# A two-layer attention trunk: layer 0's opening in five rounds instead of four, with 1024 merge-gate columns moved into it

## The chip, the cores and the metric

The kernel runs on one core of one Trainium2 chip. The metric is device time in microseconds (us) for one execution; the median of 3 runs of the kernel before is 2167.09 us (2164.69 to 2167.59). The engines are called PE (TensorE), DVE (VectorE), ACT (ScalarE), POOL (GpSimd) and SP (SyncE, which issues nearly all loads here).

## The reference, cut to what matters

Two layers (DEPTH = 2) act on x of 256 rows and 2048 features. Each layer does, in fp32:

```
mod = c @ w_ada + b_ada                      # one row; shift, scale, gate of 2048 each
u = layer_norm(x) * (1 + scale) + shift      # "adaLN"
proj = u @ w_in                              # split into the inputs of three branches and merge_logit
o_a, o_b, o_c = MLA, forgetting and stick-breaking attention on parts of proj
branches = (o_n * silu(g_n)) @ w_branch[n]   # n = 0, 1, 2
merged = sum over n of sigmoid(merge_logit[n]) * branches[n]
x = layer_norm(ALPHA * x + gate * (merged @ w_out)) * ln_g + ln_b
```

So the scale and shift must be summed from w_ada (2048 x 4096 for these two) before the first product of u with w_in, and they are needed feature by feature: feature tile k (128 features, 16 tiles) of u needs only the 128 columns of shift and scale that belong to it.

## The kernel before

An fp32 product is made of three on PE (`three`, lines 264 to 266): both operands are split into a high and a low part, ACT rounds the weights to `whi` (line 235), DVE subtracts for `wlo` (line 236), and PE adds hi*hi, hi*lo and lo*hi. The rows stand in two tiles t of 128. Weights come in pieces of 1 MiB through the four buffers `raw` of the pool wpool; the products of 512 columns are summed in PSUM banks `acc`, small things in two banks `att`.

**The opening of layer 0** (lines 601 to 710) has to fetch shift and scale while it works. It takes the feature tiles four at a time, in rounds q = 0 to 3. `ada_pieces(q, ...)` fetches the 1024 columns of shift and scale for four tiles in 8 pieces of 1 MiB (`raw_s`, line 623). DVE adds each of the 16 rows of a partition, times c, into `ada_s` (`accumulate`, lines 332 and 334), 16 sums of 1024 elements. For the first round, pieces 1, 3 and 5 are summed on PE instead, c as the stationary operand (line 635). Then PE sums over partitions against a column of ones (line 645), DVE adds the bias (`mod`, line 647), and `modulate` transposes the normalised rows `xn`, applies shift and scale on ACT (line 418) and splits the result into `uhi` and `ulo` (lines 421 and 422).

In each round, the tiles that are ready are multiplied with 3912 columns of w_in: two units of the product `first` (1024 columns, PSUM kept open over all rounds) and six blocks by `group_piece` (lines 653 to 684): two of 420 columns (`sum_b`), four of 512, which are the merge gate of branch 0 (`merged`). A block's PSUM result is copied to SBUF by ACT in round 0 (line 679) and added by DVE after that (line 681). The pieces of the next round's shift and scale are interleaved with this work, and the last block of a round is held back behind the next tiles' modulation.

**After it** come the MLA projections (`cqh` times w_uq and w_ukv), the eight MLA heads (`scores`, line 509; `attention_head`, lines 473 to 481; `attend`, lines 487 to 500), the transposes and splits of the heads' outputs (`transposed_split`, line 518, giving `yhi` and `ylo`), and the branch products with `yhi`. The heads use two PSUM banks in turn: scores, then transposed probabilities, then output. In layer 0, `merge_gate(l, 1, 0, ...)`, the first 1024 columns of branch 1's merge gate, is called right behind the MLA attention and does not depend on it:

```
            if l == 0 and n < 2:
                ahead = sig_tile(("ada", "sig")[n])
                sigs[1, n] = merge_gate(l, 1, n, ahead)
```

A scheduler sets the order of the instructions on each engine when the kernel is built, and each engine then runs its list in that order. It may move later work ahead of earlier work where buffers allow.

Of the kernel before, what the change touches and what calls it, by code (L numbers as in the profile page):

```python
# [43 lines left out]
def trunk(  # L44
# [202 lines left out]
    def half_pairs(raw):  # L247

        pairs = []
        for j in range(2):  # L250
            hi = wpool.tile([P, 2, 512], F32R, tag="whi", name="whi")
            lo = wpool.tile([P, 2, 512], F32R, tag="wlo", name="wlo")
            split_weights(raw[:, 2 * j:2 * j + 2], hi, lo)
            pairs += [(hi[:, 0], lo[:, 0]), (hi[:, 1], lo[:, 1])]
        return pairs
# [138 lines left out]
    def normalise_row(src, dst, t, mean):  # L394

        nm = small.tile([P, 1], F32, tag="nm", name="nm")
        nc.vector.tensor_scalar(nm, mean, -1.0, None, op0=ALU.mult)
        ss = small.tile([P, 1], F32, tag="ss", name="ss")
        nc.scalar.activation(dst, src[:, t], AF.Square, bias=nm, accum_out=ss)
        rs = rsqrt(ss, LN_EPS, 1.0 / D)  # L400
        nc.vector.tensor_tensor(out=nm, in0=nm, in1=rs, op=ALU.mult)
        for i in range(4):
            s = slice(i * 512, (i + 1) * 512)
            if i % 2 == 0:
                state["xn"] = nc.vector.tensor_scalar(
                    dst[:, s], src[:, t, s], mean, rs, op0=ALU.subtract, op1=ALU.mult)
            else:
                nc.scalar.activation(dst[:, s], src[:, t, s], AF.Identity, bias=nm, scale=rs)

    def modulated(l, xt_n, k0, um):  # L410

        ps = att_tile().rearrange("p (k s) -> p k s", k=4)
        for j in range(4):
            nc.tensor.transpose(ps[:, j], xt_n[:, (k0 + j) * P:(k0 + j + 1) * P], ident)
        sh, sc = mods[l][:, 0], mods[l][:, 1]
        for j in range(4):
# [7 lines left out]
    def modulate(l, xn, uhi, ulo, k0, t):  # L424
        um = tmp.tile([P, 4, P], F32, tag="t512", name="um")
        modulated(l, xn[t], k0, um)
        split_act(um, uhi[t][:, k0:k0 + 4], ulo[t][:, k0:k0 + 4])
# [118 lines left out]
    for l in range(DEPTH):  # L546
# [57 lines left out]
        if l == 0:  # L604
            sum_b = big.tile([P, NT, 2, 420], F32, tag="qT", name="sum_b")
            groups = []
            for h, parts in enumerate(([(win, CH, 420)], [(win, CH + 420, 412), (win, F0, H)])):
                groups.append((parts, [sum_b[:, t, h] for t in range(NT)],
                               lambda t, s, h=h: evac_a1(t, h, s)))
            for h in range(4):  # L610
                groups.append(([(win, M0 + h * 512, 512)], (h, ),
                               lambda t, s: nc.scalar.activation(s, s, AF.Tanh, scale=0.5)))

            ada_s = big.tile([P, 2, 2, 512], F32, tag="ada", name="ada_s")

            def ada_pieces(q, on_pe):
                acc = ada_s[:, q % 2]
                rows, merge_rows = {}, []

                def piece(u):  # L620
                    raw = wpool.tile([P, 2, 2, 512], F32, tag="raw", name="raw_s")
                    for m in range(2):
                        nc.sync.dma_start(
                            out=raw[:, :, m],
                            in_=w_ada[0].rearrange("(p k) n -> p k n", p=P)[
                                :, 2 * u:2 * u + 2, m * D + q * 512:m * D + (q + 1) * 512])
                    for j in range(2):
                        kk = 2 * u + j
                        if u not in on_pe:
                            accumulate(acc, raw[:, j], kk)  # L630
                            continue
                        for m in range(2):
                            if kk == 2 * on_pe[0]:
                                rows[m] = acc_tile()
                            nc.tensor.matmul(rows[m][:1], c_sb[:, kk:kk + 1], raw[:, j, m],
                                             start=kk == 2 * on_pe[0], stop=kk == 2 * on_pe[-1] + 1)
                            if kk == 2 * on_pe[-1] + 1:
                                merge_rows.append(m)
                    if u == 7:
                        for m in merge_rows:  # L640
                            nc.vector.tensor_tensor(out=acc[:1, m], in0=acc[:1, m], in1=rows[m][:1], op=ALU.add)
                        ps = att_tile()
                        for m in range(2):
                            for k in range(4):
                                nc.tensor.matmul(ps[:, 4 * m + k:4 * m + k + 1], acc[:, m, k * P:(k + 1) * P], ones,
                                                 start=True, stop=True)
                        nc.vector.tensor_tensor(
                            out=mods[0][:, :, 4 * q:4 * q + 4], in0=ps[:, :8].rearrange("p (m k) -> p m k", m=2),
                            in1=bT[0][:, :2, 4 * q:4 * q + 4], op=ALU.add)

                return [lambda u=u: piece(u) for u in range(8)]

            def group_piece(q, parts, sums, done):
                if len(sums) == 1:
                    sums = [merged[:, t, sums[0] * 512:(sums[0] + 1) * 512] for t in range(NT)]
                raw = wpool.tile([P, 4, 512], F32, tag="raw", name="raw_g")
                w = 0
                for src, c0, n in parts:
                    nc.sync.dma_start(
                        out=raw[:, :, w:w + n],  # L660
                        in_=src[q * 512:(q + 1) * 512, c0:c0 + n].rearrange("(k p) n -> p k n", p=P))
                    w += n
                pairs = []
                for j in range(2):
                    hi = wpool.tile([P, 2, 512], F32R, tag="whi", name="whi")[:, :, :w]
                    lo = wpool.tile([P, 2, 512], F32R, tag="wlo", name="wlo")[:, :, :w]
                    nc.scalar.activation(hi, raw[:, 2 * j:2 * j + 2, :w], AF.Copy)  # L667
                    nc.vector.tensor_tensor(  # L668
                        out=lo, in0=raw[:, 2 * j:2 * j + 2, :w], in1=hi.bitcast(F32), op=ALU.subtract)
                    pairs += [(hi[:, 0], lo[:, 0]), (hi[:, 1], lo[:, 1])]  # L670
                for t in range(NT):
                    ps = acc_tile()[:, :w]
                    for j, (hi, lo) in enumerate(pairs):
                        ah, al = uhi[t][:, 4 * q + j], ulo[t][:, 4 * q + j]
                        nc.tensor.matmul(ps, ah, hi, start=j == 0, stop=False)  # L675
                        nc.tensor.matmul(ps, ah, lo, start=False, stop=False)  # L676
                        nc.tensor.matmul(ps, al, hi, start=False, stop=j == 3)  # L677
                    if q == 0:
                        nc.scalar.activation(sums[t], ps, AF.Copy)
                    else:  # L680
                        nc.vector.tensor_tensor(out=sums[t], in0=sums[t], in1=ps, op=ALU.add)  # L681
                    if q == 3:
                        done(t, sums[t])

            for i, f in enumerate(ada_pieces(0, (1, 3, 5))):
                f()
                if i == 0:
                    for t in range(NT):
                        nc.sync.dma_start(out=xt[:, t], in_=x_rows[:, t])
# [365 lines left out]
```

## Time and profile before

| | |
|---|---|
| median of 3 runs | 2167.09 us |
| the profiled execution's own time | 2165.88 us |
| its span, first to last instruction | 2164.2 us |
| mean granted PE clock | 0.989 |
| PE busy | 2083.5 us, 96% |
| DVE busy | 1419.8 us, 66% |
| ACT busy | 985.2 us, 46% |
| moved by DMA | 481.05 MB, mean 222 GB/s |

A line of the timeline has the start in us, the duration, the engine, the line of the code, the operation, what it writes and reads, a count, and in brackets the idle time ahead of it and what ended that. A busy time overlaps where one matmul starts before the last has drained, so a product's price is read from start to start. A line of the stretches has the stretch, its length, then each engine's busy time (with the count) for PE, PEld (weight loads), DVE, ACT and POOL, and at the end the granted clock, the DMA share and GB/s. A group's line has busy time, mean ns of one, and the idle time before it. A wait's line has us in total, how often, and the longest.

### The profile page before, as it was taken

Reading aid. Unit: us, or ns where it says so; the run is one execution under the profiler, and the core shown is the slowest. Engines: PE = TensorE matmul, PEld = TensorE weight load, DVE = VectorE, ACT = ScalarE, POOL = GpSimd, SP = SyncE. Lnnn points to the kernel's source line nnn. Section 1 sums busy time; section 2 is a strip of 40 time slices with the busy share of each in tenths; the row PEclk is TensorE's granted clock in tenths of the full one; section 3 lists DMA queues with packets and bytes.
Section 4 is the critical chain, followed back from the end, with each engine's and each line's share of the span. In section 5 each row is a group of like instructions: output and inputs, shape, how many; then the busy total and the mean of one; then the engine's idle time right before and its main releaser. Section 6 shows DMA issues by size and latency. Waiting matters only on the chain. (4 is left out here: it accounts for less than half of the span.)

```text
span 2164.2 us, 24761 instructions
## 1 busy us (share of the span) xinstructions
PE 2083.5 (96%) x9568; PEld 1694.0 (78%) x9568; DVE 1419.8 (66%) x1951; ACT 985.2 (46%) x1289; POOL 14.3 (1%) x71
## 2 busy tenths in 40 slices
PE   4999999999999999999999999999999999999996
PEld 2777878888788888787848888888778888878885
DVE  6798855676658767876666755555665544466566
ACT  4435644344453445634435644444444444464441
POOL 0000000000000000000000000000000000000000
PEclk8999999999999999999999999999999999999998
DMA  8997545787648877788425646666655555555652
GB/s 313 329 330 264 175 129 174 269 299 291 207 148 298 315 262 279 281 296 308 159 106 187 224 136 233 233 229 219 232 175 175 181 193 191 195 175 195 193 196 97
DMA packets 139894, 481.05 MB, mean 222 GB/s; under 512 B 14704, under 2 KB 18944, under 8 KB 129536
## 3 DMA queue, kind: packets, MB, share of 16 engines
q1 hardware_dynamic: 135344, 464.69, 62.1%
q0 software_dynamic: 2080, 14.70, 1.7%
q8 instruction: 75, 1.23, 0.2%
q10 hardware_dynamic: 2352, 0.08, 0.1%
q14 instruction: 43, 0.35, 0.0%
HBM read 475.21 MB, written 4.23 MB: 222 GB/s over the span
## 5 line engine op out<-in xcount | busy, mean ns | idle before, releaser
L236 DVE TENSOR_TENSOR wlo<-raw,whi 128x1024 fp32r<-128x1024 f32 (+2 forms) x622 | 751.0, 1212 | 556.2 <-ACT whi L235 555.4
L235 ACT ACTIVATE whi<-raw 128x1024 fp32r<-128x1024 f32 (+2 forms) x622 | 650.4, 1050 | 770.6 <-PE acc L266 719.0
L265 PE MATMUL acc<-wlo,uhi 128*128 128x512 f32 (+1 forms) x1824 | 719.1, 394 | 0.0
L264 PE MATMUL acc<-whi,uhi 128*128 128x512 f32 (+1 forms) x1824 | 714.1, 394 | 3.8 <-ACT whi L235 3.5
L266 PE MATMUL acc<-whi,ulo 128*128 128x512 f32 (+1 forms) x1824 | 714.4, 392 | 0.0
L264 PEld LDWEIGHTS acc<-whi,uhi 128*128 128x128 f32 x1824 | 343.6, 189 | 71.1 <-ACT whi L235 4.0
L265 PEld LDWEIGHTS acc<-wlo,uhi 128*128 128x128 f32 x1824 | 344.2, 189 | 66.1 <-DVE wlo L236 0.3
L266 PEld LDWEIGHTS acc<-whi,ulo 128*128 128x128 f32 x1824 | 344.1, 189 | 66.0
L264 PE MATMUL acc<-whi,yhi 128*128 128x512 f32 x384 | 149.5, 389 | 0.0
L266 PE MATMUL acc<-whi,ylo 128*128 128x512 f32 x384 | 149.4, 389 | 0.0
L265 PE MATMUL acc<-wlo,yhi 128*128 128x512 f32 x384 | 149.4, 389 | 0.0
L334 DVE SCALAR_TENSOR_TENSOR ada_acc<-raw_ada,c_sb,ada_acc 128x2048 f32<-128x2048 f32 x60 | 140.7, 2346 | 0.1
L264 PE MATMUL acc<-whi,mhi 128*128 128x512 f32 x240 | 93.8, 392 | 2.1 <-ACT mhi L198 2.0
L265 PE MATMUL acc<-wlo,mhi 128*128 128x512 f32 x240 | 94.1, 392 | 0.0
L266 PE MATMUL acc<-whi,mlo 128*128 128x512 f32 x240 | 94.0, 392 | 0.0
L266 PEld LDWEIGHTS acc<-whi,ylo 128*128 128x128 f32 x384 | 72.1, 188 | 15.0
L264 PEld LDWEIGHTS acc<-whi,yhi 128*128 128x128 f32 x384 | 72.1, 188 | 14.9
L265 PEld LDWEIGHTS acc<-wlo,yhi 128*128 128x128 f32 x384 | 72.1, 188 | 14.9
L676 PE MATMUL acc<-wlo,uhi 128*128 128x512 f32 (+1 forms) x192 | 74.4, 390 | 6.5 <-DVE wlo L668 6.3
L675 PE MATMUL acc<-whi,uhi 128*128 128x512 f32 (+1 forms) x192 | 72.6, 387 | 5.3 <-DVE sum_b L681 2.2
L667 ACT ACTIVATE whi<-raw_g 128x1024 fp32r<-128x1024 f32 (+1 forms) x48 | 46.3, 1002 | 59.1 <-DMA raw_g<-in_w_in_dram 49.0
L677 PE MATMUL acc<-whi,ulo 128*128 128x512 f32 (+1 forms) x192 | 72.8, 383 | 0.0
(258 smaller groups left out, 1827.6 us busy)
## 6 DMA issues: line engine op xcount, KB each, us to landing
raw<-in_w_in_dram SPq DMA_DIRECT2D x223, 1024.0 KB, 5.0
raw_ada<-in_w_ada_dram SPq DMA_DIRECT2D x64, 1024.0 KB, 4.9
raw<-in_w_branch_dram SPq DMA_DIRECT2D x48, 1024.0 KB, 5.5
raw_s<-in_w_ada_dram SPq DMA_DIRECT2D x64, 512.0 KB, 5.4
raw<-in_w_out_dram SPq DMA_DIRECT2D x24, 1024.0 KB, 5.6
raw_g<-in_w_in_dram SPq DMA_DIRECT2D x16, 1024.0 KB, 6.4
raw<-in_w_in_dram SPq DMA_DIRECT2D x8, 832.0 KB, 4.5
raw<-in_w_uq_dram SPq DMA_DIRECT2D x8, 768.0 KB, 4.9
```

The source lines that it names most:

```text
L235: nc.scalar.activation(hi, raw, AF.Copy)
L236: state["dve"] = nc.vector.tensor_tensor(out=lo, in0=raw, in1=hi.bitcast(F32), op=ALU.subtract)
L264: nc.tensor.matmul(ps, ah, hi, start=k == 0, stop=False)
L265: nc.tensor.matmul(ps, ah, lo, start=False, stop=False)
L266: nc.tensor.matmul(ps, al, hi, start=False, stop=k == n - 1)
L334: nc.vector.scalar_tensor_tensor(out=acc, in0=raw, scalar=col, in1=acc, op0=ALU.mult, op1=ALU.add)
L667: nc.scalar.activation(hi, raw[:, 2 * j:2 * j + 2, :w], AF.Copy)
L675: nc.tensor.matmul(ps, ah, hi, start=j == 0, stop=False)
L676: nc.tensor.matmul(ps, ah, lo, start=False, stop=False)
L677: nc.tensor.matmul(ps, al, hi, start=False, stop=j == 3)
```

## The change

The opening takes the feature tiles in five rounds of 2, 2, 4, 4 and 4, with 4936 columns instead of 3912: the first 1024 columns of branch 1's merge gate are two more blocks of 512 (`early`). The call of `merge_gate(l, 1, 0, ...)` behind the MLA attention falls away; the one for the other half, behind branch 1's attention, stays.

Shift and scale of the first two tiles (4 MiB in 4 pieces, runs of 1 KiB instead of 2 KiB) are summed on PE alone: the weights are the stationary operand and one column of c moves, 64 products of one column, whose result is already laid out over partitions. x is loaded ahead of them. For the later rounds DVE sums as before, over 512 elements for the two tiles of the second round and 1024 for four.

In the first round the two tiles `um0` are multiplied in plain fp32, with no split, for `first` and for the six merge-gate blocks in pairs (`two_blocks`); the two blocks of 420 columns take tiles 0 to 3 together in the second round (`four_tiles`). The second round's pairs are split. Because a block of 512 columns is now closed five times instead of four, DVE adds it four times instead of three.

The core of the diff (the rewriting of `normalise` and of `half_pairs` for narrower blocks is left out):

```diff
+            for h in range(2):
+                blocks.append(Block([(win, M0 + D + h * 512, 512)], lambda t, h=h: early[:, t, h * 512:(h + 1) * 512],
+                                    gate_done(lambda t, h=h: early_gate(t, h))))
...
+            def two_blocks(k0, pair):
+                raw = weight_load([p for b in pair for p in b.parts], k0 // 2)
+                split = weight_pairs(raw, CH) if k0 else None
+                for t in range(NT):
+                    for h, b in enumerate(pair):
+                        ps, s = acc_tile(), slice(h * 512, (h + 1) * 512)
+                        for j in range(2):
+                            if split:
+                                hi, lo = split[j]
+                                three(ps, uhi[t][:, k0 + j], ulo[t][:, k0 + j], hi[:, s], lo[:, s], j, 2)
+                            else:
+                                nc.tensor.matmul(ps, um0[t][:, j], raw[:, j, s], start=j == 0, stop=j == 1)
+                        b.evac(t, ps, 2)
...
+            for t in range(NT):
+                nc.sync.dma_start(out=xt[:, t], in_=x_rows[:, t])
+            column = {(m, j): acc_tile() for m in range(2) for j in range(2)}
+            for i in range(4):
+                raw, kks = ada_load(0, 2, i)
+                for a, kk in enumerate(kks):
+                    for (m, j), ps in column.items():
+                        nc.tensor.matmul(ps[:, :1], raw[:, a, m, j * P:(j + 1) * P], c_sb[:, kk:kk + 1],
+                                         start=kk == 0, stop=kk == KT - 1)
...
+            rounds = ((0, 2), (2, 2), (4, 4), (8, 4), (12, 4))
+            for r, (k0, n) in enumerate(rounds):
+                if n == 4:
+                    work = [lambda u=u: first.unit(u) for u in (k0 // 2, k0 // 2 + 1)]
+                    work += [lambda b=b: four_tiles(k0, b) for b in blocks]
+                else:
+                    work = [first_plain if r == 0 else lambda: first.unit(1)]
+                    work += [lambda b=b: two_blocks(k0, b) for b in pairs_of]
+                    if r == 1:
+                        work += [lambda b=b: four_tiles(0, b) for b in blocks[:2]]
...
-            if l == 0 and n < 2:
-                ahead = sig_tile(("ada", "sig")[n])
-                sigs[1, n] = merge_gate(l, 1, n, ahead)
+            if l == 0 and n == 1:
+                sigs[1, 1] = merge_gate(l, 1, 1, sig_tile())
```

The order of the instructions shows what this moves. The first place is PE's list from the start to the first products with w_in (`raw_s` holds pieces of shift and scale, `c_sb` is c, `xn` the normalised rows). Before:

```order
L635 MATMUL acc<-raw_s,c_sb 1x512 x12
L645 MATMUL att<-ones,ada_s 128x1 x4
L414 MATMUL att<-ident,xn 128x128 x2
L645 MATMUL att<-ones,ada_s 128x1 x4
L414 MATMUL att<-ident,xn 128x128 x6
L264 MATMUL acc<-whi,uhi 128x512 x4
```

The same place of PE's list in the changed kernel, where `um_309` and `um_315` are the two row tiles in plain fp32:

```order
L718 MATMUL acc<-c_sb,raw_s 128x1 x32
L411 MATMUL att<-ident,xn 128x128 x2
L718 MATMUL acc<-c_sb,raw_s 128x1 x24
L411 MATMUL att<-ident,xn 128x128 x2
L718 MATMUL acc<-c_sb,raw_s 128x1 x8
L317 MATMUL acc<-raw,um_309 128x512 x2
L317 MATMUL acc<-raw,um_315 128x512 x2
```

The sums over partitions by ones are gone from the start, and the first products take `raw` and `um` directly instead of split parts.

The second place is DVE's list where one round's modulation (`mod`) meets the next round's adaLN sums (`ada_s`) and weight splits (`wlo`). Before, between round 0's modulation and its first splits:

```order
L332 TENSOR_SCALAR ada_s<-raw_s,c_sb 128x1024
L647 TENSOR_TENSOR mod_149<-att,bT_85 128x2x4
L334 SCALAR_TENSOR_TENSOR ada_s<-raw_s,c_sb,ada_s 128x1024
L422 TENSOR_TENSOR ulo<-um,uhi 128x512
L236 TENSOR_TENSOR wlo<-raw,whi 128x1024
```

In the changed kernel, at the modulation of tiles 2 and 3 on DVE:

```order
L334 SCALAR_TENSOR_TENSOR ada_s<-raw_s,c_sb,ada_s 128x2x256 x15
L332 TENSOR_SCALAR ada_s<-raw_s,c_sb 128x1024
L334 SCALAR_TENSOR_TENSOR ada_s<-raw_s,c_sb,ada_s 128x1024
L667 TENSOR_TENSOR mod_149<-att,bT_85 128x2x2
L419 TENSOR_TENSOR ulo<-um,uhi 128x256 x2
L236 TENSOR_TENSOR wlo<-raw,whi 128x1024
```

Both sums of the first piece for tiles 4 to 7 now stand ahead of the modulation of tiles 2 and 3; before, one sum stood there.

The third place is PE's list in a head of the MLA attention of layer 0: scores (`kT,qT` and `peT`), transposes of the probabilities (`sm`), output (`v,pt`). Before, from the end of the first head's scores, with products of the merge gate (`uhi`, `ulo`) between, of which the rows for the middle are left out here because they repeat:

```order
L264 MATMUL acc<-whi,uhi 128x512
L487 MATMUL att<-ident,sm 128x128
L265 MATMUL acc<-wlo,uhi 128x512
L487 MATMUL att<-ident,sm 128x128 x2
L266 MATMUL acc<-whi,ulo 128x512
L264 MATMUL acc<-whi,uhi 128x512
L265 MATMUL acc<-wlo,uhi 128x512
L266 MATMUL acc<-whi,ulo 128x512
L264 MATMUL acc<-whi,uhi 128x512
L492 MATMUL att<-v,pt 128x128
```

PE's list for the first head in the changed kernel:

```order
L506 MATMUL att<-peT 128x256
L484 MATMUL att<-ident,sm 128x128 x3
L489 MATMUL att<-v,pt 128x128
L490 MATMUL att<-v,pt 128x128
L491 MATMUL att<-v,pt 128x128
L506 MATMUL att<-kT,qT 128x128
L506 MATMUL att<-peT 128x128
```

All products of the merge gate have left the heads, and the next head's scores stand behind the output of the one before. From the first branch product on, the order of PE is that of before.

214 lines of the change are left out of this document (105 added, 109 removed).

## The prediction

> **What bounds the kernel now.** I read the page's busy times first, then the stretches of the span, then TensorE's waits.
>
> ```profile
> PE 2083.5 (96%) x9568; PEld 1694.0 (78%) x9568; DVE 1419.8 (66%) x1951; ACT 985.2 (46%) x1289; POOL 14.3 (1%) x71
> PE   4999999999999999999999999999999999999996
> 0.00:250.00 250.00, 210.18 (x925) 165.45 (x926) 199.46 (x330) 119.04 (x175) 5.01 (x53) 0.96 0.83 289
> 250.00:500.00 250.00, 250.00 (x1204) 205.44 (x1202) 161.38 (x227) 113.17 (x161) 0.00 (x0) 1.00 0.63 222
> ```
>
> TensorE (PE) is the bound: 81 us idle in 2164, and 40 of them in the first 250. After that it has no gap at all up to 500, so work put there costs its full PE time. The opening is the one place where PE could take more. Its waits and its marks in the timeline:
>
> ```profile
> PE acc L635 <- DMA raw_s<-in_w_ada_dram: 10.9, 2, 9.2
> PE acc L676 <- DVE wlo L668: 6.3, 9, 2.1
> 46.33 2.08 PE L264 MATMUL acc<-whi,uhi 128*128 128x512 f32 x4 [3.55 <-ACT whi L235]
> 89.61 1.84 PE L645 MATMUL att<-ones,ada_s 128*128 128x1 f32 x16
> 246.47 0.33 PE L264 MATMUL acc<-whi,cqh 128*128 128x384 f32 x1
> 280.92 0.39 PE L509 MATMUL att<-kT,qT 128*128 128x128 f32 x2
> 328.26 0.60 PE L518 MATMUL att<-ident,g 128*128 128x128 f32 x4
> 346.02 0.39 PE L264 MATMUL acc<-whi,yhi 128*128 128x512 f32 x1
> 365.75 0.39 PE L264 MATMUL acc<-whi,yhi 128*128 128x512 f32 x1
> ```
>
> The first real product is at 46.33. At 89.61 the modulation of tiles 4 to 7 is summed; I call this M. At 246.47 all input products of layer 0 that the opening holds are done (E). At 346.02 the first branch product starts (Y). From Y to the end the program's order is the same in both kernels, so those 2164.2 - 346.0 = 1818.2 us stay, and I need M, M to E and E to Y.
>
> **Prices.** 29 triples of products lie between the last two rows above: 19.73/87 = 0.227 us for one 512-column product, 0.68 for the three of an fp32 product. Others:
>
> ```profile
> 65.37 0.35 PE L676 MATMUL acc<-wlo,uhi 128*128 128x420 f32 x1
> 66.49 0.35 PE L676 MATMUL acc<-wlo,uhi 128*128 128x420 f32 x1
> 1089.48 10.03 PE L1004 MATMUL acc<-held,m_last 128*128 128x512 f32 x23
> L334 DVE SCALAR_TENSOR_TENSOR ada_s<-raw_s,c_sb,ada_s 128x1024 f32<-128x1024 f32 x15 | 19.2, 1281 | 0.2
> L236 DVE TENSOR_TENSOR wlo<-raw,whi 128x1024 fp32r<-128x1024 f32 x4 | 4.7, 1220 | 0.3 <-ACT whi L235 0.3
> L668 DVE TENSOR_TENSOR wlo<-raw_g,whi 128x840 fp32r<-128x840 f32 x4 | 3.9, 1026 | 0.0
> L681 DVE TENSOR_TENSOR merged<-merged,acc 128x512 f32<-128x512 f32 x6 | 4.1, 683 | 1.1 <-PE acc L677 1.1
> L681 DVE TENSOR_TENSOR sum_b<-sum_b,acc 128x420 f32<-128x420 f32 x4 | 2.4, 592 | 2.2 <-PE acc L677 2.2
> L422 DVE TENSOR_TENSOR ulo<-um,uhi 128x512 fp32r<-128x512 f32 x2 | 1.4, 690 | 1.1 <-ACT uhi L421 1.1
> 91.30:141.50 50.20, 46.93 (x223) 38.67 (x223) 44.56 (x47) 20.14 (x28) 0.00 (x0) 1.00 0.94 326
> ```
>
> A 420-column product: 1.12/6 = 0.187. A plain fp32 product: 10.03/23 = 0.436, less than its triple. The column sums of L645 took 1.84/16 = 0.115 each. The last row is one round of before: in 50.2 us PE is busy 46.9, DVE 44.6, ACT 20.1. ACT's part of every edit lies under the others by that row, so I cost it at nothing; if DVE and ACT swapped roles it would not.
>
> **Part 1: the start and the two small rounds (M).** The first tiles' adaLN takes 4 MiB instead of 8, summed by 64 column products (64 x 0.115 = 7.4 us, between landings), so the first product should come near 28 us instead of 46. But the next rounds wait for more data. Counting SP's loads up to the last piece of tiles 4 to 7, I get 26.8 MiB now and 26.6 before: equal. The plain products save 32 x (0.68 - 0.436) = 7.8 us of PE and 8 splits of weights, at a place where PE waits for data and modulation anyway, so I book nothing for them.
>
> ```profile
> 91.49 0.17 DVE L647 TENSOR_TENSOR mod<-att,bT 128x8 f32<-128x8 f32 x1 [1.59 <-PE att L645]
> 92.70 0.75 DVE L332 TENSOR_SCALAR ada_s<-raw_s,c_sb 128x1024 f32<-128x1024 f32 x1
> 94.69 0.69 DVE L422 TENSOR_TENSOR ulo<-um,uhi 128x512 fp32r<-128x512 f32 x1
> 0.00:20.00 20.00, 4.55 (x7) 0.93 (x8) 7.61 (x48) 8.64 (x8) 5.01 (x53) 1.00 0.83 280
> 31.00:37.00 6.00, 0.00 (x0) 0.00 (x0) 5.42 (x5) 0.00 (x0) 0.00 (x0) 0.79 1.05 393
> ```
>
> Bytes alone allow 28.1 MB at 280 GB/s to 20 us and 393 after it: 20 + 22.5/0.393 = 77 us. DVE does not. Its queue has the first two sums of the next adaLN piece ahead of the modulation of tiles 2 and 3 (the order rows above the prediction). That piece ends the 15th MiB, 15.7 MB: 20 + 10.1/0.393 = 46, plus 0.75 + 1.28, and a buffer wait or two: 49. From the modulation to the split of the activations before took 94.69 - 91.49 = 3.2 (52). Round 2 gives DVE 16 adaLN sums (0.75 + 15 x 1.28 = 20.0), 8 splits of 1.22 (9.8), 4 of 1.03 (4.1), 12 adds of 0.683 (8.2): 42 us, of which 39 still stand ahead of M. With 2 us idle M is 93. Bounds: 88 (nothing idle, data on time) and 98 (the 5.6 us that DVE was idle in the row of a round, and more). So M moves +3.4, from 89.6 to 93, although the first product comes 18 us sooner. The loads in 1 KiB runs instead of 2 KiB are inside these bounds: no row here has such runs. [...]
>
> **Part 2: M to E, with 1024 more columns.** Before, 456 products at 0.227, 144 at 0.187 and some 9 us of sums and transposes make 139.5 us of PE in 156.9: 17.4 over. After, the order has 576 and 168: 130.8 + 31.4 + 9 = 171. What comes over it? DVE's round of four tiles becomes 20.0 + 16 x 1.22 + 4 x 1.03 + 12 x 0.683 + 4 x 0.592 + 1.4 = 55.5 us (44.6 before), against 55 of PE. They are level, so I expect no less over-run than before: 18, together 189. Bounds: 12 over (PE-bound, clean) and 26 (DVE leads). M to E grows by 189 - 156.9 = 32.
>
> **Part 3: E to Y, without the merge gate.** 192 products at 0.227 leave, 43.6 us of PE. They were not idle filler there: the order had them between the steps of the eight MLA heads. Now a head's steps stand one behind another. From one head of before, and the end of another:
>
> ```profile
> 310.50 0.39 PE L509 MATMUL att<-kT,qT 128*128 128x128 f32 x2
> 312.01 0.29 DVE L473 CUSTOM_DVE_ANT_0 sm<-att,m_mla 128x128 f32<-128x128 f32 x1 [0.70 <-PE att L509]
> 312.69 0.17 DVE L476 TENSOR_SCALAR mx<-mx 128x2 f32<-128x2 f32 x1
> 312.89 0.40 ACT L479 ACTIVATE sm<-sm,mx 128x128 f32<-128x128 f32 x1 [3.22 <-DVE mx L476]
> 313.69 0.19 ACT L479 ACTIVATION_READ_ACCUMULATOR sm<-sm,mx 128x1 f32 x1
> 302.52 0.38 PE L487 MATMUL att<-ident,sm 128*128 128x128 f32 x2
> 303.00 0.49 ACT L489 ACTIVATE pt<-att 128x384 f32<-128x384 f32 x1 [0.71 <-PE att L487]
> 303.54 0.49 PE L492 MATMUL att<-v,pt 128*128 128x128 f32 x2
> 304.31 0.39 PE L509 MATMUL att<-kT,qT 128*128 128x128 f32 x2
> ```
>
> Scores to the first reduction 1.51, to the exponentials 0.88, to their end 0.99, a step to the transposes 0.05, transposes to the next head's scores 1.79: 5.2 us, where heads with filler took (328.26 - 280.92)/8 = 5.9. Only 0.7 a head is gained; 8 x 5.2 = 41.6 replace 47.3. In front, four products fall (0.9). Behind, the 17.8 us from 328.26 to 346.02, filled by what remained of the gate, become about 2.5: four transposes (0.6), their split on ACT (like the 0.49 of pt) and DVE (like the 0.69 of ulo), and the steps between. Eight transposes (8 x 0.11) move behind Y. Saved: 0.9 + 5.7 + 15.3 - 0.9 = 21, with 18 to 23 as bounds (a split late, or the next scores started early). So 43.6 us of PE work leave and about 22 come back as idle time.
>
> **Sum.** 93 + 189 + 78.6 + 1818.2 = 2178.8 where 2164.2 stood: +15. The profiled execution took 2165.88, 1.2 below the median 2167.09; I put the same +15 on the median: 2182. The lower bounds together give -1.6 + 26.4 - 23 = +2, the upper ones +8.4 + 40.4 - 18 = +31.
>
> **Rivals.** (a) Faster: the early rounds run as fast as data come. M would be 77 to 78, and with 12 over-run the sum is -12 + 26 - 21 = -7: 2160. It decides at M = 78.6, where the sum is zero with my other terms. For it: 393 GB/s was measured; against it: the 39 us of DVE that start only after tiles 2 and 3 are modulated. Chance 0.04. (b) No change: all lower bounds come together, +2, within 0.2% (about 4 us, what a measurement can tell): 2169. Chance 0.06. (c) Slower still: PE's clock falls in the bare heads, where PE works at most 2.7 of 5.2 us (1.51 + 0.38 + 0.77 by the rows of a head).
>
> ```profile
> 14.00:18.00 4.00, 1.90 (x3) 0.32 (x4) 0.31 (x2) 3.35 (x3) 0.00 (x0) 1.00 1.04 395
> 46.00:49.00 3.00, 2.67 (x6) 2.17 (x7) 2.69 (x3) 3.00 (x5) 0.00 (x0) 0.50 0.39 152
> ```
>
> After the 6 idle us of 31 to 37 the granted clock went to 0.79 in that stretch and was still 0.50 at 46 to 49; at 48% busy (14 to 18) it stayed 1.00. Halved, each head has up to 2.7 us more, 8 x 2.7 = 21: 2203. The longest gap in a bare head is about 1.9 us, so I give it 0.10. [...] (d) The change does not free the later place: excluded, since the order shows it.
>
> **Numbers.** My forecast (over 4 us slower, clock up) has 0.80, with (c) slower 0.90, same 0.06, faster 0.04. Its own range is 2172 to 2194, since the bounds seldom come all together. Down to 2171 and up to 2200 it takes in half of (b), and the upper bounds (2198) with a part of (c).
>
> **What would show it.** Right: first plain products near 28 us; M between 88 and 98 with PE waiting on modulation and DVE before it; E near 282; then eight heads 5.2 us apart with nothing between their steps, PE waiting on the exponentials, and Y near 361. Wrong: M below 82, or E below 268, or heads that overlap.

## The result and the profile after

| | before | after |
|---|---|---|
| median | 2167.09 us (2164.69 to 2167.59) | 2204.85 us (2203.48 to 2205.64) |
| profiled execution | 2165.88 us | 2204.25 us |
| its span | 2164.2 us | 2202.5 us |
| mean granted clock | 0.989 | 0.987 |

The ratio is 1.0176, with a 95% interval of 1.0160 to 1.0192: 37.8 us slower, where I forecast 15, and outside my range. First the busy times, TensorE's slices and the two quarter-milliseconds of after:

```profile
PE 2116.3 (96%) x9632; PEld 1721.2 (78%) x9632; DVE 1423.8 (65%) x1977; ACT 982.7 (45%) x1287; POOL 14.3 (1%) x71
PE   7899996999999999999999999999989999999996
0.00:250.00 250.00, 227.12 (x981) 180.47 (x982) 184.41 (x293) 103.46 (x147) 5.01 (x53) 0.99 0.87 293
250.00:500.00 250.00, 228.13 (x1038) 186.79 (x1037) 152.46 (x269) 110.28 (x171) 0.00 (x0) 0.95 0.51 175
```

TensorE's idle time in the first quarter fell from 40 us to 23, as the change would have it, but the second, which had none, now has 22, and a granted clock of 0.95. Total PE busy time *rose* by 33 us for the same mathematics: some of the work got dearer. The waits and the marks M, E and Y in the timeline of after:

```profile
PE att L484 <- ACT sm L476: 16.3, 19, 2.3
PE att L489 <- ACT pt L486: 7.7, 12, 0.9
PE acc L718 <- DMA raw_s<-in_w_ada_dram: 7.1, 1, 7.1
PE acc L265 <- DVE wlo L236: 7.0, 13, 2.1
14.73 13.78 PE L718 MATMUL acc<-c_sb,raw_s 128*128 128x1 f32 x64 [7.13 <-DMA raw_s<-in_w_ada_dram]
28.84 10.24 PE L718 MATMUL acc<-c_sb,raw_s 128*128 128x1 f32 x48
39.40 3.41 PE L718 MATMUL acc<-c_sb,raw_s 128*128 128x1 f32 x16
43.12 9.66 PE L317 MATMUL acc<-raw,um 128*128 128x512 f32 x16 [0.31 <-ACT um L415]
52.62 13.90 PE L684 MATMUL acc<-raw,um 128*128 128x512 f32 x32
66.35 0.95 PE L665 MATMUL att<-ones,ada_s 128*128 128x1 f32 x8
111.06 1.84 PE L665 MATMUL att<-ones,ada_s 128*128 128x1 f32 x16
292.62 0.33 PE L264 MATMUL acc<-whi,cqh 128*128 128x384 f32 x1
327.05 0.39 PE L506 MATMUL att<-kT,qT 128*128 128x128 f32 x2
382.70 0.51 PE L264 MATMUL acc<-whi,yhi 128*128 128x512 f32 x1
```

Three readings. The 64 column sums hold PE from 14.73 to 42.8, and after the first landing they wait for no transfer: PE's own work keeps the first product at 43.12. They stand there as 64 + 48 + 16 = 128 records, and the 8 plain products of L317 as 16: the trace writes two records for one plain fp32 matmul. And the two longest waits are those of the heads (ACT's exponentials and the copy of pt), which before were filled. Against the forecast:

| stage | before | forecast | after | error of the forecast |
|---|---|---|---|---|
| start to M | 89.6 | 93 | 111.1 | +18.1 |
| M to E | 156.9 | 189 | 181.6 | -7.4 |
| E to Y | 99.6 | 78.6 | 90.1 | +11.5 |
| Y to end | 1818.2 | 1818.2 | 1819.8 | +1.6 |

### The profile page after: what moved, and what is told of

Its sections match the earlier page's. It is cut to its first block, busy times and chain, and to the rows that moved or that the text cites. A ratio compares the mean times of both kernels' runs of the same rounds, so it can differ in the third digit from the quotient of the medians.

```text
span 2202.5 us, 24933 instructions
## 1 busy us (share of the span) xinstructions
PE 2116.3 (96%) x9632; PEld 1721.2 (78%) x9632; DVE 1423.8 (65%) x1977; ACT 982.7 (45%) x1287; POOL 14.3 (1%) x71
## 5 line engine op out<-in xcount | busy, mean ns | idle before, releaser
L236 DVE TENSOR_TENSOR wlo<-raw,whi 128x1024 fp32r<-128x1024 f32 (+2 forms) x610 | 736.1, 1211 | 543.2 <-ACT whi L235 542.4
L235 ACT ACTIVATE whi<-raw 128x1024 fp32r<-128x1024 f32 (+2 forms) x610 | 637.8, 1050 | 781.1 <-PE acc L266 723.1
L265 PE MATMUL acc<-wlo,uhi 128*128 128x512 f32 (+1 forms) x1984 | 777.9, 393 | 7.2 <-DVE wlo L236 7.0
L266 PE MATMUL acc<-whi,ulo 128*128 128x512 f32 (+1 forms) x1984 | 771.8, 390 | 0.0
L265 PEld LDWEIGHTS acc<-wlo,uhi 128*128 128x128 f32 x1984 | 373.8, 188 | 82.7 <-DVE wlo L236 13.3
L264 PEld LDWEIGHTS acc<-whi,uhi 128*128 128x128 f32 x1984 | 372.9, 188 | 78.1 <-DVE merged L618 3.2
L266 PEld LDWEIGHTS acc<-whi,ulo 128*128 128x128 f32 x1984 | 373.8, 188 | 69.8
L334 DVE SCALAR_TENSOR_TENSOR ada_s<-raw_s,c_sb,ada_s 128x1024 f32<-128x1024 f32 (+1 forms) x60 | 68.9, 1149 | 6.8 <-DMA raw_s<-in_w_ada_dram 5.8
L476 ACT ACTIVATE sm<-sm,mx 128x128 f32<-128x128 f32 x64 | 28.5, 446 | 78.9 <-DVE mx L473 78.9
L236 DVE TENSOR_TENSOR wlo<-raw_g,whi 128x1024 fp32r<-128x1024 f32 (+1 forms) x52 | 59.7, 1161 | 4.2 <-ACT whi L235 4.2
```

Of the source, the lines that this page charges most:

```text
L235: nc.scalar.activation(hi, raw, AF.Copy)
L236: state["dve"] = nc.vector.tensor_tensor(out=lo, in0=raw, in1=hi.bitcast(F32), op=ALU.subtract)
L264: nc.tensor.matmul(ps, ah, hi, start=k == 0, stop=False)
L266: nc.tensor.matmul(ps, al, hi, start=False, stop=k == n - 1)
L334: nc.vector.scalar_tensor_tensor(out=acc, in0=raw, scalar=col, in1=acc, op0=ALU.mult, op1=ALU.add)
L476: nc.scalar.activation(sm[:, a:b], sm[:, a:b], AF.Exp, bias=mx[:, t:t + 1], scale=scale, accum_out=rs[:, t:t + 1])
```

## The experiments

I had two theories for the two positive errors. P (prices): the column sums and the plain products cost PE about twice what I booked. C (clock): the granted clock falls in the bare heads. The expectations set two others against them: D (M is set by data and DVE alone, whatever PE's prices) and L (the chain of steps in a head is longer than I worked out, whatever the clock). Each run below is compared with runs of the kernel before on the same chip; M, E and Y are read as above.

**e1: the 1024 columns back behind the MLA heads, the five rounds kept.**

```diff
-            for h in range(2):
-                blocks.append(Block([(win, M0 + D + h * 512, 512)], ...))
-            pairs_of = [blocks[i:i + 2] for i in (2, 4, 6)]
+            pairs_of = [blocks[i:i + 2] for i in (2, 4)]
-            if l == 0 and n == 1:
-                sigs[1, 1] = merge_gate(l, 1, 1, sig_tile())
+            if l == 0 and n < 2:
+                sigs[1, n] = merge_gate(l, 1, n, sig_tile(("ada", "sig")[n]))
```

> The 1024 columns of branch 1's merge gate go back behind the MLA attention; five rounds, column sums and plain products stay. Marks: M (sums of tiles 4 to 7) was 89.6 before and 111.1 after, M to E 156.9 and 181.6, E to Y 99.6 and 90.1. If the early prices on PE were wrong (column sum 0.43 us, plain product 0.87 us, theory P), the first round has 24 plain products instead of 32, 7 us less, and the second 24 split products less: M near 98, still later than before; M to E about 158, E to Y 99 to 100, together 2174 to 2178, slower than before by some 9. If M is set by data and DVE alone (theory D), M falls to 88 to 92 with the smaller rounds and the total is within 4 of before.

Measured: 2178.44 us, ratio 1.0065 [1.0050, 1.0080], span 2174.5; M 102.75, M to E 155.4, E to Y 99.5. So moving the columns costs 28.0 of the 38.3 us of span, and the rounds with their sums and plain products some 10. M is still 13 us late without the columns, 5 us later than P had it and far from D's 88 to 92.

**e2: the first round's products split in three, as in the other rounds.**

```diff
-                modulated(0, xn[t], 0, um0[t])
+                modulate(0, xn, uhi, ulo, 0, t, 2)
-                split = weight_pairs(raw, CH) if k0 else None
+                split = weight_pairs(raw, CH)
```

> The first round's tiles are split and multiplied three times like the others, instead of once in plain fp32. Theory P: 32 x 0.87 = 28 us of PE become 96 x 0.227 = 22, so M comes 3 to 6 us earlier (105 to 108) and the total is 2199 to 2202. If plain products are the cheaper ones, as I had booked them (0.436), M comes 8 us later, 119, and the total is 2213. Theory D: M unchanged or later by the 8 splits (10 us of DVE).

Measured: 2206.26 us, ratio 1.0190 [1.0173, 1.0207]; M 114.4. Neither price came true in M (105 to 108 by P, 119 by my booking); 3.4 us later lies within what D allowed. The first product is 2.5 us later (45.62, behind a split), and the first round is no shorter, 24.0 us to the modulation of tiles 2 and 3 in place of 23.2. The plain products are dearer than I booked (0.86 us each in after, (66.35 - 52.62)/16), and putting split ones in their place did not help M.

**e3: the first two tiles' adaLN summed on DVE, as in the other rounds.**

```diff
-                        nc.tensor.matmul(ps[:, :1], raw[:, a, m, j * P:(j + 1) * P], c_sb[:, kk:kk + 1],
-                                         start=kk == 0, stop=kk == KT - 1)
+            for f in ada_pieces(0, 2, 1):
+                f()
```

> The first two tiles' adaLN is summed by DVE (16 sums of 512 elements, about 0.7 us each) and the ones column, as in the later rounds, instead of 64 column products on PE. Theory P: the 27 us of column products set the first product at 43; without them it comes near 29, 4 MiB of data and 11 us of DVE being done by then, and M falls by 8 to 14, to 97 to 103; total 2191 to 2197. Theory D: DVE has 11 us more to do and M stays at 108 to 112.

Measured: 2195.18 us, ratio 1.0139 [1.0124, 1.0154], span 2192.1. Two marks of its timeline:

```profile
33.17 2.07 PE L317 MATMUL acc<-raw,um 128*128 128x512 f32 x2 [0.55 <-ACT um L415]
101.27 0.95 PE L665 MATMUL att<-ones,ada_s 128*128 128x1 f32 x8
```

The first product comes 9.95 us sooner, M 9.8, the end 10.4. The column sums on PE are what held the start, as P has it; D, with M at 108 to 112, is out for them.

**e4: the change with products that nothing reads among the steps of the MLA heads**, five of 512 columns behind the scores and three ahead of the copy of pt, so that PE need not rest.

```diff
                     S = scores(qT, kT, h, [(qpT[:, h // 2], kz[:, h % 2])])
+                    fill(5)
...
+        fill(3)
         pt = tmp.tile([P, 3 * P], F32, tag="pt", name="pt", bufs=2)
```

> Eight products whose result nobody reads are added to each of layer 0's MLA heads (64 in all, 14.6 us at 0.227), to keep PE busy between the steps. Theory C (the clock was halved in the bare heads, 0.72 to 0.78 granted): the heads go from 6.7 us to 5.2 to 5.6, the clock stays at 1.00, E to Y falls from 90 to 79 to 83, and the total to 2194 to 2198 although there is more work. Theory L (the chain of steps is longer than I worked out, whatever the clock): the heads stay at 6.7 or grow, total 2204 to 2215.

Measured: 2194.47 us, ratio 1.0138 [1.0123, 1.0153], span 2194.2; E to Y 81.3. Stretches of the heads, first of after, then of this run (the column behind POOL's is the granted clock):

```profile
327.00:360.00 33.00, 21.49 (x85) 16.57 (x84) 9.17 (x41) 8.05 (x26) 0.00 (x0) 0.78 0.10 34
360.00:376.00 16.00, 11.46 (x45) 9.26 (x44) 3.79 (x18) 2.95 (x10) 0.00 (x0) 0.72 0.00 1
```

```profile
330.00:342.00 12.00, 12.00 (x69) 9.79 (x67) 4.85 (x19) 3.46 (x11) 0.00 (x0) 1.00 0.28 91
342.00:354.00 12.00, 12.00 (x65) 9.45 (x64) 3.99 (x21) 3.12 (x11) 0.00 (x0) 1.00 0.01 1
```

More work on PE, and the heads are faster: E to Y is 8.8 us shorter. C holds, and this run shows it a second way. The scheduler put the 64 products among the first five heads, so that the last three still stand bare. The last of those products, the scores of the three bare heads, and the transposes behind the last head:

```profile
355.16 0.71 PE L486 MATMUL acc<-uhi 128*128 128x512 f32 x2
356.81 0.39 PE L515 MATMUL att<-kT,qT 128*128 128x128 f32 x2
362.10 0.39 PE L515 MATMUL att<-kT,qT 128*128 128x128 f32 x2
368.05 0.64 PE L515 MATMUL att<-kT,qT 128*128 128x128 f32 x2
374.98 1.39 PE L524 MATMUL att<-ident,g 128*128 128x128 f32 x5
```

The three take 5.29, 5.95 and 6.93 us; the granted clock is 1.00 in 354 to 366 and 0.72 in 366 to 372 (0.86 over 354 to 376), and the score pairs above take 0.39, 0.39 and 0.64 us. So a bare head at full clock took 5.3 us here, close to the 5.2 I had worked out, and one like those of after (6.83 from 346.80 to 353.63) only once the clock has fallen again. That rules out L. Eight heads at 5.29 would be 42.3 us where after has 53.9: by this estimate the clock is the whole 11.5 us of the error. The last two heads together are 2.3 us longer than two at 5.29, which is most of what e4 leaves of it.

**e5 and e6: a merge gate among the heads again, the early columns kept.** e6 is the change with the gate of branch 1's second half moved up to the MLA heads and one of branch 2 to the next attention; e5 has e3's edit too.

```diff
-            if l == 0 and n == 1:
-                sigs[1, 1] = merge_gate(l, 1, 1, sig_tile())
+            if l == 0 and n < 2:
+                sigs[n + 1, 1 - n] = merge_gate(l, n + 1, 1 - n, sig_tile(("sig", "ylo")[n]))
...
-                    e = big.tile([P, 4, 3 * P], F32, tag="ylo", name="e")
+                    e = big.tile([P, 4, 3 * P], F32, tag="ylo" if l else "sig", name="e")
```

> The change with two edits: the first two tiles' adaLN sums go through VectorE as for the other tiles, and layer 0's MLA attention and the one after it each get a merge gate among their heads again (1024 columns of branch 1 in the first, of branch 2 in the second), so that no head stands bare and the early 1024 columns stay. Each gate is some 43.5 us of TensorE that leaves the stretch behind. Theory (prices): the start is that of the run with sums on VectorE (M near 101, E near 284), E to Y is that of before (99.6), and the rest is shorter by one gate, 1818 - 43 = 1775; span near 2158 to 2162, time near 2160 to 2164, so 0.2 to 0.4% below the kernel before. Rival: VectorE, which splits the early columns' weights and now the sums as well, binds the filled heads; then E to Y is 105 or more and the time is level with before, 2167 to 2172.

> The change with the start as it is, but a merge gate among the heads of layer 0's first two attentions again, as in the kernel before (branch 1's second half, then branch 2's first half). Theory (bare heads cost clock and time): a gate of some 43.5 us leaves the stretch behind Y and fills heads that cost 90 bare and 99.6 filled, so the span falls by about 34 us, to 2168 or so, time near 2170. Rival (the gate's columns only move, and their time with them): E to Y goes to 90 + 43 = 133 and the time stays near 2204.

Measured: e5 2196.56 us, ratio 1.0142 [1.0127, 1.0158]; e6 2206.23, 1.0187 [1.0173, 1.0201]. Both expectations of a gain failed, and not in the way of the rivals named: in e6 E to Y is 99.5 with PE busy throughout and the clock at 1.00. The time came back later. Layer 0's third attention, in after and in e6:

```profile
900.00:956.00 56.00, 52.96 (x274) 42.65 (x273) 49.75 (x68) 36.45 (x46) 1.58 (x3) 1.00 0.73 268
```

```profile
900.00:956.00 56.00, 29.88 (x122) 24.38 (x123) 26.56 (x54) 24.09 (x30) 1.05 (x2) 0.60 0.22 79
```

The third attention had had a gate among its heads all along, in the tile "sig", which I had overlooked; my edit gave that tile to e. I had moved the hole, not closed it.

**e10: e5, with a gate in all three attentions.** The third works on two heads at a time, so that z and e share one tile and "sig" is free for the last gate.

```diff
-                for hb in range(2):
+                hn = 4 if l else 2
+                for hb in range(H // hn):
...
+                    else:
+                        z, e = z[:, :2], z[:, 2:]
```

> The run with VectorE sums and the gates shifted, with one more edit: layer 0's third attention works on two heads at a time, so that its tiles fit one buffer and the last merge gate (branch 2, second half) can run among its heads. In the run before it the bare heads had only moved: its third attention stood bare with the granted clock at 0.50 in 940 to 950. Theory (a bare attention costs some 33 us wherever it stands, by clock and by waits): the time falls by 30 to 35 against the run before it (2196.6), to 2162 to 2167. Rival (two heads at a time make the third attention wait on ScalarE and VectorE itself): the time falls by less than 20, to 2177 or above.

Measured: 2163.51 us, ratio 0.9991 [0.9982, 1.0000], span 2163.4: 33 us less than e5, as expected, and level with the kernel before. (The clock of 0.50 in 940 to 950 that the expectation names is e6's; e5 reads 0.64 over 900 to 956.) The same stretch of this run:

```profile
900.00:956.00 56.00, 50.55 (x259) 40.40 (x257) 47.36 (x64) 40.27 (x51) 1.05 (x2) 1.00 0.64 225
```

**e7 and e9: is it the clock that makes a column sum dear?** e7 puts one plain product of 256 columns ahead of each four column sums; e9 puts ten of them, back to back, into PE's idle time ahead of the first.

```diff
+                    nc.tensor.matmul(spare[:, :SEQ], raw[:, a, 0, :P], tri, start=True, stop=True)
                     for (m, j), ps in column.items():
```

```diff
+            for _ in range(10):
+                nc.tensor.matmul(spare[:, :SEQ], ident, tri, start=True, stop=True)
             column = {(m, j): acc_tile() for m in range(2) for j in range(2)}
```

> The change with 16 more plain fp32 products of 256 columns, one ahead of each group of four column sums, whose result nothing reads. Theory (cold clock): TensorE keeps the half clock through 28 us of one-column products since these are too short to raise it; with wide products among them a column sum falls from 0.43 to about 0.23 us, the 16 products cost 0.44 each, the first feature product starts near 37 to 41 in place of 43.1, M is near 104 to 109. Rival (a one-column product costs 0.43 at any clock): 7 us are added, the first feature product starts at 50 or later, M is 117 or more, the time some 7 us above that of the change.

> The change with ten plain fp32 products of 256 columns (identity by a constant, result unread) back to back on TensorE from about 7 us, where it stood idle until the first adaLN rows came at 14.7. Theory A (wide products raise the clock, and a busy TensorE keeps it): the 64 column sums run at 0.23 us each, the first feature product comes near 32 where its data allow, M near 100, time near 2194. Theory B (one-column products neither raise the clock nor hold it): the first few sums run at 0.23, the rest at 0.43 again, the first feature product stays between 39 and 44, M 107 to 112, time 2200 to 2205. Theory C (a one-column product costs 0.43 where its stationary comes from a transfer, at any clock): all sums at 0.43 from the first, feature products at 43 to 45.

e7 measured: 2217.27 us, ratio 1.0240 [1.0226, 1.0254]; first product at 56.4, M 123.8. My theory's numbers failed: the 16 added products put 13.3 us on the start, 0.83 each, and the sums stayed dear. The rival's bounds (first product at 50 or later, M at 117 or more) are the ones met, and e9 had to decide:

```profile
19.10 3.41 PE L720 MATMUL acc<-c_sb,raw_s 128*128 128x1 f32 x16
22.38 1.20 PE L718 MATMUL acc<-tri,raw_s 128*128 128x256 f32 x2
```

(22.38 - 19.10)/16 is 0.205 us a record, two records a sum. e9 measured: 2202.93 us, ratio 1.0172 [1.0158, 1.0185]; first product at 40.46, M 108.6, so theory B. Its timeline and stretches tell why (the counts are records, two for a sum):

```profile
7.41 7.32 PE L715 MATMUL acc<-tri,ident 128*128 128x256 f32 x20
...
16.17 3.92 PE L721 MATMUL acc<-c_sb,raw_s 128*128 128x1 f32 x33 [0.83 <-DMA raw_s<-in_w_ada_dram]
19.95 5.90 PE L721 MATMUL acc<-c_sb,raw_s 128*128 128x1 f32 x27
25.71 0.67 PE L411 MATMUL att<-ident,xn 128*128 128x128 f32 x2
```

```profile
14.70:20.00 5.30, 4.43 (x39) 4.35 (x38) 2.97 (x18) 3.49 (x9) 0.00 (x0) 0.98 1.10 350
20.00:25.00 5.00, 5.00 (x25) 5.00 (x25) 2.16 (x12) 2.80 (x4) 0.00 (x0) 0.50 1.10 348
```

From start to start, (19.95 - 16.17)/33 = 0.115 us a record, and from 20 on (25.71 - 19.95)/27 = 0.213: the same work at twice the price, with the granted clock at 0.50 and PE busy 5.00 of 5.00 us. So it is the clock (the one-column product is not dear by itself), and one-column products did not hold it up. In e7 products of 256 columns in a third of the time did not raise it either: 0.205 us a record among them. That refutes the rival of e7: a one-column product took 0.23 us (two records) with the granted clock at 0.98.

**e8 and e12: the five rounds alone.** e8 is e1 and e3 together; e12 is that and e2. The edits are those above.

> Five rounds of 2, 2, 4, 4, 4 tiles alone: the sums of the first two tiles on VectorE, the early 1024 columns back behind the heads of the first attention. What is left of the change is the smaller first rounds and the plain products of the first. Theory (each part is worth its own term): of the run with the columns back (span 2174.5) the VectorE sums take 8 to 10 us off, span 2164 to 2166, level with the kernel before (2164.2). Rival (smaller rounds start earlier and are a gain that the sums hid): span 2158 or less. Rival (plain products of the first round are a net cost): span 2170 or more.

> The five rounds alone with sums on VectorE and the early columns behind the heads of the first attention, as in the run of that kind with span 2171.5 and M at 97.9, and the first round's products split in three as in the other rounds (0.68 us each) in place of plain fp32 (0.87 us each). Theory (the plain products are what the five rounds still cost): 32 products save 6 us, M is 91 to 93, span near 2165, level with the kernel before. Rival (what they cost lies in their small rounds, in which TensorE waits for the next splits and sums whatever the products take): M stays between 96 and 101, span 2169 to 2175.

Measured: e8 2172.87 us, ratio 1.0032 [1.0019, 1.0045], M 97.9; e12 2171.86, ratio 1.0026 [1.0016, 1.0036], M 95.4, between the bounds of both sides and nearer the rival's. Smaller rounds start the first product at 32.9 (e8) in place of 46.3 and still lose 8 us up to M. PE in the second round of each, e8 first:

```profile
56.00:90.00 34.00, 26.10 (x82) 17.28 (x80) 27.30 (x28) 9.63 (x12) 0.00 (x0) 0.85 0.89 309
```

```profile
56.00:90.00 34.00, 25.82 (x94) 18.71 (x94) 29.35 (x30) 9.49 (x12) 0.00 (x0) 0.90 0.88 299
```

PE is idle for 8 of 34 us with either kind of products, at a granted clock of 0.85 and 0.90, while DVE and the DMA are at 80 to 90%. What was gained at the start is waited for in the second round. Split products in place of the plain ones take 2.6 us off M here, where in e2 they added 3.4.

**e11: the early columns alone, on the kernel before.** Its own four rounds of four tiles and its own sums, eight blocks a round, and a gate in each of the three attentions as in e10, the third on two heads at a time.

```diff
+            for h in range(2):
+                groups.append(([(win, M0 + D + h * 512, 512)], [early[:, t, h * 512:(h + 1) * 512] for t in range(NT)],
+                               lambda t, s, h=h: early_done(t, s, h)))
...
-            if l == 0 and n < 2:
-                sigs[1, n] = merge_gate(l, 1, n, ahead)
+            if l == 0:
+                nxt = ((1, 1), (2, 0), (2, 1))[n]
+                sigs[nxt] = merge_gate(l, *nxt, sig_tile(("sig", "ylo", "sig")[n]))
```

> The kernel before with the early 1024 columns alone: its own four rounds of four tiles and its own sums, eight blocks in each round in place of six, and a merge gate among the heads of each of layer 0's three attentions (the third on two heads at a time). Theory (each part is worth its own term: the early columns ride at 34.5 us of 43.5 in the rounds, the small rounds with VectorE sums cost 7): span 2164 - 9 = 2155, time 2155 to 2162, below the kernel before by 0.2 to 0.5%. Rival (the early columns only pay with the small rounds, since the first four tiles are bound by transfers): level with the kernel before or above, 2166 to 2175.

Measured: 2157.49 us (2155.91 to 2158.24), ratio 0.9960 [0.9947, 0.9972]: 8 us below the kernel before, and 47 below the change. Its marks M, E and Y:

```profile
97.47 0.72 PE L658 MATMUL att<-ones,ada_s 128*128 128x1 f32 x6
278.38 0.33 PE L264 MATMUL acc<-whi,cqh 128*128 128x384 f32 x1
377.87 0.39 PE L264 MATMUL acc<-whi,yhi 128*128 128x512 f32 x1
```

Against before, the stages move by +7.9, +24.0, -0.1 and, from Y to the end (2155.8 - 377.9 = 1777.9), -40.3. The early columns take 31.9 us in the opening; the gate that no longer has to run later gives 40.3 back. What the third attention on two heads at a time is worth by itself, no run shows. Against e10 (2163.51), which has the same gates and columns, the five rounds with sums on DVE cost 6 us.

## Why the prediction was wrong, and where it was right

**Part 1 failed in the price of the column sums, and in what waits for them.** I took 1.84/16 for one sum of L645. Those 16 records are 8 sums, so one is 0.23, and 64 are 14.7 us, not 7.4. Then came the clock: 0.43 each, 27 us in all. "Between landings" failed with it: the first product came at 43.1 and not near 28.

My M did not hang on that product, though, but on the 15th MiB landing at 46, with "a buffer wait or two" to 49. This is the step that failed: a piece keeps its buffer until PE has summed it, and the next load waits for the buffer. The waits of SP's queue up to 75 us in after, and DVE's first sum of that piece:

```profile
SPq L224 <- PE acc L718: 11.9, 2, 6.1
SPq L648 <- PE acc L718: 10.4, 2, 6.7
66.03 0.75 DVE L332 TENSOR_SCALAR ada_s<-raw_s,c_sb 128x1024 f32<-128x1024 f32 x1 [2.83 <-DMA raw_s<-in_w_ada_dram]
```

The queue stood for 22.3 us behind buffers that the column sums held, and the sum that I had at 46 waited for its data until 66.03. PE was no earlier: the plain products fill it without a gap from 43.12 to 66.35, and the sums over partitions for tiles 2 and 3 stand behind them. So the late start carried over to M, where I had taken M to be independent of it. In e3 the first product is at 33.2 and M 9.8 us sooner, so 10 of the 18 us are the sums on PE. The other 8: the first product is 5 us later than 28 even then, and the first round takes 24.5 us from there to the modulation of tiles 2 and 3, where I had 21. From that modulation to M I forecast 44 (49 to 93); after shows 44.7 and e3 43.6. That step was right in size; DVE is busy for 38.8 of the 44.7 us and PE for 38.9, so that it was DVE's list that set it is not shown.

The plain product was mis-priced in the same way. The 23 records of L1004 are 11.5 products, so one is 0.87 us: dearer than its triple at 0.68, not cheaper by 0.24. The first round's 32 took 28 us of PE and not 14. I had booked no gain for them, and by e2 and e12 split ones would move M by about 3 us one way or the other, so most of this error stayed outside the sum. The count would have shown it in the kernel before: its order has the sums of L645 eight at a time, where the trace has sixteen.

**Part 2 was right in kind and 7.4 us too high.** 1024 more columns cost 24.7 us, below my lower bound of 26.4. One stretch of after:

```profile
111.00:292.60 181.60, 176.13 (x832) 147.60 (x831) 157.06 (x239) 95.00 (x135) 0.00 (x0) 1.00 0.80 272
```

PE is idle for 5.5 us there and busy for 5 more than the 171 I had added up: 10.6 over, where I put 18. With DVE busy for 157 of 181.6 us the two got less into each other's way than in before, where PE is idle for 9.7 us in this stage and I had read 17.4 over. My lower bound, 12 over, was already too high. In e11 the same stage grows by 24.0.

**Part 3 failed in the clock: rival (c), to which I gave 0.10, came true,** though not in its full size. From 327.05 to the end of the last head at 380.95 there are 53.9 us, 6.7 a head, where I had 5.2; the way to the first head took 34.4 as before, and the end behind the last head took 1.8, where I had 2.5. The priced 21 us of (c) were an upper bound; e4 takes 8.8 off, and by the estimate from its bare head at full clock the clock is worth 11.6. That (c)'s 2203 lies next to the measured 2204.85 is luck: it holds neither the 18.1 us of Part 1 nor the -7.4 of Part 2. The reason I gave against it fell: no gap in these heads is over 1.74 us, and the clock fell in the first of them (1.00 in 327 to 330, 0.69 in 330 to 334):

```profile
327.27 0.39 PE L506 MATMUL att<-peT 128*128 128x128 f32 x2
...
330.26 0.33 PE L484 MATMUL att<-ident,sm 128*128 128x128 f32 x1 [1.74 <-ACT sm L476]
...
333.21 0.63 PE L506 MATMUL att<-kT,qT 128*128 128x128 f32 x2
333.64 0.64 PE L506 MATMUL att<-peT 128*128 128x128 f32 x2
```

The scores of the first head are 0.22 us from product pair to product pair (327.05, 327.27), those of the second 0.43. The clock does not stay down either, but swings within each head:

```profile
339.00:342.00 3.00, 3.00 (x14) 2.74 (x13) 0.61 (x2) 0.00 (x0) 0.00 (x0) 0.54 0.00 0
342.00:345.00 3.00, 1.09 (x5) 0.34 (x3) 0.98 (x6) 1.17 (x5) 0.00 (x0) 1.00 0.00 0
345.00:348.00 3.00, 2.64 (x11) 2.63 (x12) 0.61 (x2) 0.31 (x1) 0.00 (x0) 0.53 0.00 0
```

It is down (0.54, 0.53) while PE works through outputs and scores, and up again (1.00) while PE mostly waits, busy for 1.09 of 3 us. My other reason, that the clock stayed at 1.00 at 48% busy in 14 to 18 of before, was misread. Records of L635 there and later:

```profile
16.90 1.92 PE L635 MATMUL acc<-raw_s,c_sb 128*1 128x512 f32 x2
27.15 3.59 PE L635 MATMUL acc<-raw_s,c_sb 128*1 128x512 f32 x8 [1.66 <-DMA raw_s<-in_w_ada_dram]
```

Two took 1.92 us at 16.90 (0.96 each), eight took 3.59 at 27.15 (0.45 each). By these durations the clock was at half at 16.90, and the row did not show it.

**Right:** the direction; that the later place is freed and the order behind Y is unchanged (1819.8); that part of the gate's 43.6 us come back as idle time in the bare heads (PE is idle for 19.1 of the 90.1 us from E to Y, where I had about 22); the length of the second round (44.7 us, where I had 44). My "what would show it" named PE waiting on the exponentials, and that is the first row of the waits. Its other signs failed: the first plain product near 28, M up to 98, heads 5.2 us apart, Y near 361.

What stays open: whether the share of wide products decides the clock (a third of the time did not raise it in e7), why it swung within the bare heads, and whether data, DVE or the clock costs the small rounds most.

## What to carry to other kernels

Before a duration is divided by a count, compare the count in the trace with the count in the program: here two records made one fp32 product, and each plain fp32 price came out at half. Before a load is timed by bytes alone, ask which engine still holds its buffer. Work that filled the waits of the heads cost less there than its PE time: a gate of 43.6 us made E to Y only 9.5 us longer, with the granted clock at 1.00 from E to Y in before and at 0.72 to 0.78 in the bare heads of after. Whoever takes such work away must put other work there, and must follow the buffers to see that the hole isn't just moved. Of a change in several parts, run each alone: here one part was worth 8 us and lay hidden under a bare attention (33), column sums on PE (10) and small rounds (6 to 8).

## What the runs showed of the hardware

- In the bare heads of after, with TensorE recorded as 65 to 72% busy and no gap over 1.74 us, the granted clock swung between half and full (0.53 to 1.00 in stretches of 3 us, 0.72 to 0.78 on average), and a head took 6.8 us; at full clock a bare head took 5.3 (e4). It also fell to half under one-column products at 100% recorded busy (e9: 0.98 in 14.7 to 20, 0.50 in 20 to 25), some 5 us after the last wide product.
- 28 us of one-column products at the start of after left it at half: 0.213 us a record from 14.73 to 28.38, and the last 16 took 3.41. So did 42 us in which products of 256 columns took a third of the time (e7, 0.205 a record). Under products of 512 columns it rose, in about 5 us: the 16 records from 43.12 took 9.50 us and the 32 behind them 13.73, so some 6 of the 16 ran at the double price. In e9, with the first such product at 40.46, the same 16 took 8.56 us, and the row itself reads 0.63 in 40 to 45 and 1.00 in 45 to 50; in before, with the first product of w_in at 46.33, it reads 0.50 in 46 to 49, 0.57 in 49 to 52 and 1.00 in 52 to 56.
- The profile's clock row reads 1.00 for the first 43 us of after, though the sums there ran at 0.213 us a record like those at 0.50 in e9; in before it reads 1.00 in 14 to 18, with records at the double price (0.96 us, against 0.45 at 27.15). At the start of these two traces I took the clock from the durations and not from the row.
- A plain fp32 product of 512 columns took 0.86 us in after (13.73/16, two records each), three split ones 0.68 together in before (19.73/29).
